# A delta-rule recurrence whose triangular inverse is multiplied into the per-chunk products ahead of the chain of chunks

## Chip, cores and metric

One core of one Trainium2 chip. The metric is the device time of one execution in microseconds; three executions of the kernel before were timed, and a fourth was profiled.

## What is computed

A decoder trunk of two layers over 256 positions of width 1024, float32 in and out. The part that the change touches is the recurrence of layer 0 (8 heads of 64, state `S` of 64 x 64 a head):

```python
def step(S, inp):
    r_t, w_t, k_t, v_t, kk_t, a_t = inp
    sa = jnp.einsum('bhvk,bhk->bhv', S, -kk_t)
    S = (S * w_t[:, :, None, :] + sa[..., None] * (kk_t * a_t)[:, :, None, :]
         + v_t[..., None] * k_t[:, :, None, :])
    return S, jnp.einsum('bhvk,bhk->bhv', S, r_t)
```

The rest of layer 0 is a combined projection, a second mixer (gMLP: a layer norm over the positions' values and a 128 x 128 spatial product), the output projection and a gated feed-forward; layer 1 is attention and another feed-forward.

## The kernel before, in words

Large products run as three matmuls of split operands (`mm3`, tiles `pg`): weights arrive by SP's queue as `raw`, ScalarE makes `whi` (L246), VectorE makes `wlo` (L247). Everything else of TensorE goes to the tiles `pm`.

The recurrence is cut into 4 chunks of 64 positions, in two halves (`h` = 0, 1) of 4 heads each. `stream(h)` builds for each chunk of each head the operands `WR` (128 rows: 64 of the state's and 64 of the values' side; columns 0:64 W0, 64:128 for the outputs, 128:192 for the next state) and `BK` (columns 0:64 A, 64:192 what the solution of the triangular system is multiplied with). The 64 x 64 triangular matrix is inverted in steps: VectorE inverts 16 x 16 blocks (L177 `ftmp`, L690 to L702, tile `xx`) on data that ScalarE's queue carries through DRAM (`scrA`, L670, read back as `at`, L675; written as `scrX`, L701 and L703, read back as `XT`, L706), and the section `lev` joins blocks with four small products (`each`, `low`, L736 to L749; VectorE's COPY_PREDICATED, L742 and L743, and copies on VectorE and ScalarE). `XT`'s second half is `TI`, the inverse transposed.

Then the chain over the chunks `c`, per half: `pw` = W0 times the state, copied to `w0t` (L773); `pq` = inverse times `w0t`, copied to `qst` (L779); `pn`, the next state, from a product over 128 rows and one over 64 rows with `qst`, copied to `SV` (L787, VectorE and ScalarE one half each); `po`, the output, in the same way, copied to `oT` (L792). After every second chunk a side job (`epilogue`, tiles `sqo`, `r2e`) normalises 128 positions.

`projections()` issues the large products of the layer; between a long run of them and the output projection stands the layer norm of the second mixer (tile `vt`, L529 to L538). `drive()` decides in which order TensorE gets all this, by a clock of its own: each job says how much TensorE time a step takes, `RAT` how much of the projections is put behind it, and the table `WAIT` how long each step has to stay away from the one before. TensorE's order is kept as issued (`tc.manual_schedule`); the other engines' orders are made by the scheduler, with `PRI` as its priorities.

Of the kernel before, what the change touches and what calls it, by code (L numbers as in the profile page):

```python
# [8 lines left out]
F32 = mybir.dt.float32  # L9
# [3 lines left out]
OP = mybir.AluOpType  # L13
# [10 lines left out]
DECAY = math.exp(-0.5)  # L24


WAIT = {'s0': [0, 3402, 0, 0, 0, 0, 5130, 0, 0, 6181, 0, 1558, 0, 0, 0, 0, 29481, 1432, 0, 614, 2396, 0, 0, 1233, 677, 0, 0, 451, 317, 0, 0, 0, 98, 638, 0, 377, 334, 316, 0, 0, 528, 1719], 's1': [0, 0, 0, 19323, 0, 0, 2756, 596, 813, 0, 0, 0, 0, 29456, 711, 0, 0, 527, 0, 0, 599, 67, 0, 296, 671, 180, 0, 0, 0, 802, 275, 0, 256, 750, 589, 0, 0, 381, 499], 'v0': [], 'v1': [0, 0, 0, 0, 2188, 540], 'e00': [0, 2221, 997], 'e01': [0, 914, 2924], 'e10': [0, 957, 1874], 'e11': [0, 896, 1993], 'p': [3172, 8550]}
DSQ = (3, 5)
WARM = 16
SEGS = []  # L30
# [2 lines left out]
RAT = {'rows': 3.5, 'pk0': 0.151, 'pk1': 0.1, 'lora': 0.568, 'prod0': 1.61, 'prod1': 0.03, 'v0': 1.318, 'v1': 1.865, 'lev0': 0.3, 'lev1': 0, 'ch0': 0.116, 'ch1': 0}  # L33
# [126 lines left out]
def body(nc, tc, A, out):  # L160
# [3 lines left out]
    V, S, G, PE, SP = nc.vector, nc.scalar, nc.gpsimd, nc.tensor, nc.sync  # L164
# [3 lines left out]
    sm = ctx.enter_context(tc.tile_pool(name="sm", bufs=2))  # L168
# [3 lines left out]
    def mm(o, l, r, start=True, stop=True, shared=False):  # L172
        cnt[0] += 1
        PE.matmul(o, l, r, start=start, stop=stop, skip_group_check=shared)  # L174

    def tt(o, a, b, op, eng=None):
        (eng or V).tensor_tensor(o, a, b, op)  # L177
# [17 lines left out]
    ident, ones = C("ident", 128), C("ones", 1)  # L195
# [155 lines left out]
    def mps():  # L351
        return ps.tile([128, 512], F32, name="pm", tag="m", bufs=5)
# [43 lines left out]
    def layer_even(nxt):  # L396
# [6 lines left out]
        n = norm_new()  # L403
# [13 lines left out]
        WR = ev.tile([128, 2, 16, 192], F32, name="WR")  # L417
# [160 lines left out]
        def stream(h):  # L578
# [127 lines left out]
                    S.dma_start(XT[64 * p:64 * p + 64, w], grid(scrX[h, w], p))  # L706

            yield ("side", f"v{h}", values(h))
            yield ("sec", "lev")
            XI, TI = XT[:, 0], XT[:, 1]  # L710
            YI = chunks(t2("YI"))
# [38 lines left out]
            yield ("pe", 860, RAT[f"lev{h}"])  # L750


            yield ("need", f"val{h}")
            oT = t2("oT")
            YB[h] = [t2(f"yb{i}", F32R) for i in "hl"]

            def heads():
                for j in js:
                    for p in range(2):
                        yield j, p, slice(64 * p, 64 * p + 64), slice(64 * (j - 2 * h), 64 * (j - 2 * h) + 64)  # L760

            def pair(o, whole, half):

                for i, f in enumerate((whole, half)):
                    for j, p, q, e in heads():
                        mm(o[q, e], *f(j, p, q, e), i == 0 and j == js[0], i == 1, True)

            for c in range(4):
                pw = mps()
                for j, p, q, e in heads():  # L770
                    mm(pw[q, e], WR[:, p, 4 * j + c, 0:64], SV[:, p, j, c])
                w0 = sm.tile([128, 128], F32, name="w0t", tag="w0t", bufs=3)
                V.tensor_copy(w0, pw[:, 0:128])  # L773
                yield ("pe", 330, RAT[f"ch{h}"])
                pq = mps()
                for j, p, q, e in heads():
                    mm(pq[q, e], TI[q, 4 * (j - 2 * h) + c], w0[q, e])
                qs = sm.tile([128, 128], F32, name="qst", tag="qst", bufs=3)
                V.tensor_copy(qs, pq[:, 0:128])  # L779
                yield ("pe", 330, RAT[f"ch{h}"])  # L780
                if c < 3:
                    pn = mps()
                    pair(pn, lambda j, p, q, e: (WR[:, p, 4 * j + c, 128:192], SV[:, p, j, c]),
                         lambda j, p, q, e: (BK[q, 4 * j + c, 128:192], qs[q, e]))
                    for p in range(2):
                        q = slice(64 * p, 64 * p + 64)
                        (S.copy if p else V.tensor_copy)(SV[q, p, jsl, c + 1, :], pn[q, 0:128].rearrange("p (j n) -> p j n", j=2))  # L787
                    yield ("pe", 660, RAT[f"ch{h}"])
                po = mps()
                pair(po, lambda j, p, q, e: (SV[:, p, j, c], WR[:, p, 4 * j + c, 64:128]),  # L790
                     lambda j, p, q, e: (qs[q, e], BK[q, 4 * j + c, 64:128]))
                S.copy(oT[:, :, 64 * c:64 * c + 64], po[:, 0:128].rearrange("p (j n) -> p j n", j=2))  # L792
                yield ("pe", 660, RAT[f"ch{h}"])
                if c % 2:
                    yield ("side", f"e{h}{c // 2}", epilogue(h, c // 2, oT))

        def values(h):
            js = (2 * h, 2 * h + 1)
            jsl = slice(2 * h, 2 * h + 2)
            k_ = kx[h]  # L800
            yield ("sec", "val")

            yield ("need", f"v{h}")
            for p in range(2):
                G.memset(SV[64 * p:64 * p + 64, p, jsl, 0, :], 0.0)
            pp = mps()
            for g in range(8):
                j, c = 2 * h + g // 4, g % 4
                for p in range(2):
                    q, o_ = slice(64 * p, 64 * p + 64), slice(64 - 64 * p, 128 - 64 * p)  # L810
                    mm(pp[o_, 64 * g:64 * g + 64], v_[q, j, 64 * c:64 * c + 64], C("cent", 64)[q])
                if g % 4 == 3:
                    yield ("pe", 648, RAT[f"v{h}"])
            pv = pp.rearrange("p (j c n) -> p j c n", j=2, c=4)
            for p in range(2):
                o_ = slice(64 - 64 * p, 128 - 64 * p)
                S.copy(SV[o_, p, jsl], pv[o_])

            pg = mps()
            for i, j in enumerate(js):  # L820
                mm(pg[:, T * i:T * i + T], lora[:, 512 + 128 * j:640 + 128 * j], L[:, 1])
            S.copy(gate[:, jsl], pg.rearrange("p (a b) -> p a b", a=2))
            yield ("pe", 870, RAT[f"v{h}"])

# [397 lines left out]
```

## Time and profile before

| what | us |
|---|---|
| three timed executions | 669.67, 677.36, 678.03 (median 677.36) |
| profiled execution, its own time | 672.47 |
| its span, first to last instruction | 670.6 |
| mean granted TensorE clock of the span | 0.981 |

The span is the time from the first to the last instruction that the profile records; 1.9 us of the profiled execution lie around it. The recurrence runs beside the projections of layer 0, in the first 165 us of the span; what follows it is not touched.

### The profile page before, as it was taken

Reading aid. Unit: us, or ns where it says so; the run is one execution under the profiler, and the core shown is the slowest. Engines: PE = TensorE matmul, PEld = TensorE weight load, DVE = VectorE, ACT = ScalarE, POOL = GpSimd, SP = SyncE. Lnnn points to the kernel's source line nnn. Section 1 sums busy time; section 2 is a strip of 40 time slices with the busy share of each in tenths; the row PEclk is TensorE's granted clock in tenths of the full one; section 3 lists DMA queues with packets and bytes.
Section 4 is the critical chain, followed back from the end, with each engine's and each line's share of the span. In section 5 each row is a group of like instructions: output and inputs, shape, how many; then the busy total and the mean of one; then the engine's idle time right before and its main releaser. Section 6 shows DMA issues by size and latency. Waiting matters only on the chain.

```text
span 670.6 us, 14493 instructions
## 1 busy us (share of the span) xinstructions
PE 642.1 (96%) x5766; PEld 613.1 (91%) x5766; DVE 500.4 (75%) x904; ACT 390.6 (58%) x710; POOL 136.4 (20%) x196
## 2 busy tenths in 40 slices
PE   7998979799899999999999999999999999999995
PEld 6997767679899999999999999999999999998895
DVE  6799967647988888886656479886887888885543
ACT  6776432324666666665445467776576666664431
POOL 4100000110414444441112000001233333331000
PEclk9998999869999999999999999999999999999999
DMA  7747264202456665666666454442755555555541
GB/s 253 249 148 232 71 177 100 73 2 95 127 193 198 197 198 190 189 178 199 188 196 225 160 158 133 139 137 78 245 193 178 189 188 184 185 190 176 179 127 63
DMA packets 44915, 110.33 MB, mean 165 GB/s; under 512 B 16432, under 2 KB 18096, under 8 KB 44848
## 3 DMA queue, kind: packets, MB, share of 16 engines
q1 hardware_dynamic: 31104, 105.03, 48.6%
q10 hardware_dynamic: 13584, 3.86, 2.4%
q8 instruction: 45, 0.74, 0.4%
q0 software_dynamic: 160, 0.52, 0.3%
q14 instruction: 22, 0.18, 0.1%
HBM read 106.50 MB, written 2.90 MB: 163 GB/s over the span
## 4 chain that ended last, share of the span: by engine, by line
PE 79%; DVE 12%; DMA 3%; issue 2%; ACT 1%; POOL 1%; ACTq 1%; SPq 0%; POOLq 0%; DVEq 0%
PE pg L174 63%; PE pm L174 14%; DVE wlo L247 3%; DVE WR L177 2%; DMA scrA<-BK 1%; DVE ftmp L177 1%; PE pm L1142 1%; DVE xl L304 1%; DMA R<-xT 1%; DMA at<-scrA 1%; DMA raw<-w_up 1%; ACTq L706 0%; PE prb L174 0%; DVE BK L662 0%; POOL r L321 0%
## 5 line engine op out<-in xcount | busy, mean ns | idle before, releaser
L246 ACT ACTIVATE whi<-raw 128x1024 fp32r<-128x1024 f32 (+2 forms) x199 | 202.6, 1024 | 157.2 <-PE pg L174 77.6
L174 PE MATMUL pg<-xh,whi 128*128 128x256 f32 x1008 | 289.1, 287 | 0.4 <-ACT whi L246 0.4
L247 DVE TENSOR_TENSOR wlo<-raw,whi 128x1024 fp32r<-128x1024 f32 (+2 forms) x199 | 234.5, 1183 | 71.4 <-ACT whi L246 70.8
L174 PE MATMUL pg<-xh,wlo 128*128 128x256 f32 x1008 | 283.1, 281 | 2.0 <-DVE wlo L247 2.0
L174 PE MATMUL pg<-xl,whi 128*128 128x256 f32 x1008 | 283.1, 281 | 0.1
L174 PEld LDWEIGHTS pg<-xh,whi 128*128 128x128 f32 x1008 | 191.7, 190 | 6.1 <-issue 3.9
L174 PEld LDWEIGHTS pg<-xh,wlo 128*128 128x128 f32 x1008 | 191.5, 190 | 2.7 <-DVE wlo L247 2.6
L174 PEld LDWEIGHTS pg<-xl,whi 128*128 128x128 f32 x1008 | 193.2, 192 | 0.7 <-DVE xl L300 0.3
L177 POOL TENSOR_TENSOR y<-y 128x256 f32<-128x256 f32 x44 | 61.7, 1401 | 27.7 <-ACT y L987 26.8
L177 POOL TENSOR_TENSOR sqacc<-sqacc,sq 128x256 f32<-128x256 f32 x21 | 18.6, 887 | 166.0 <-ACT sq L312 165.5
L984 ACT ACTIVATE y<-z,pc 128x256 f32<-128x256 f32 x88 | 47.5, 587 | 3.3 <-DVE z L177 3.3
L174 PE MATMUL pg<-hh,wlo 128*128 128x256 f32 x176 | 48.6, 276 | 0.0
L174 PE MATMUL pg<-hl,whi 128*128 128x256 f32 x176 | 48.6, 276 | 0.0
L174 PE MATMUL pg<-hh,whi 128*128 128x256 f32 x176 | 48.6, 276 | 0.0
L177 DVE TENSOR_TENSOR z<-pg,rb 128x512 f32<-128x512 f32 (+1 forms) x46 | 30.5, 667 | 21.3 <-PE pg L174 21.3
L985 DVE SCALAR_TENSOR_TENSOR y<-z,pc,y 128x256 f32<-128x256 f32 x88 | 38.6, 478 | 0.8 <-ACT y L984 0.8
L986 DVE SCALAR_TENSOR_TENSOR y<-z,pc,y 128x256 f32<-128x256 f32 x88 | 38.6, 478 | 0.1
L174 PEld LDWEIGHTS pg<-hl,whi 128*128 128x128 f32 x176 | 33.0, 188 | 0.0
L174 PEld LDWEIGHTS pg<-hh,wlo 128*128 128x128 f32 x176 | 33.0, 188 | 0.0
L174 PEld LDWEIGHTS pg<-hh,whi 128*128 128x128 f32 x176 | 33.0, 188 | 0.0
L177 POOL TENSOR_TENSOR hl<-y,hh 128x256 fp32r<-128x256 f32 x42 | 31.2, 742 | 0.0
L975 POOL MEMSET z<- 128x4 f32 x44 | 4.2, 103 | 128.7 <-DVE y L986 97.4
(248 smaller groups left out, 1032.5 us busy)
## 6 DMA issues: line engine op xcount, KB each, us to landing
raw<-w_up SPq DMA_DIRECT2D x88, 512.0 KB, 3.5
raw<-w_dn SPq DMA_DIRECT2D x30, 512.0 KB, 3.5
raw<-w_qkv SPq DMA_DIRECT2D x24, 512.0 KB, 3.5
raw<-w_in SPq DMA_DIRECT2D x20, 512.0 KB, 4.8
raw<-w_dn SPq DMA_DIRECT2D x16, 448.0 KB, 3.4
raw<-ev_wo SPq DMA_DIRECT2D x8, 512.0 KB, 3.8
raw<-od_wo SPq DMA_DIRECT2D x8, 512.0 KB, 4.0
R<-xT SPq DMA_DIRECT2D x4, 256.0 KB, 4.2
```

The lines of the kernel that those rows point to most:

```text
L174: PE.matmul(o, l, r, start=start, stop=stop, skip_group_check=shared)
L177: (eng or V).tensor_tensor(o, a, b, op)
L246: S.activation(hi[:, c], raw[:, c], AF.Copy)
L247: last["lo"] = V.tensor_tensor(lo[:, c], raw[:, c], hi[:, c].bitcast(F32), OP.subtract).ins
L304: V.scalar_tensor_tensor(x[1][:, k], R[:, k], P(gname, k), x[0][:, k].bitcast(F32), op0=OP.mult, op1=OP.subtract)
L975: G.memset(z[:, :, 0:2], 0.0)
L984: S.activation(y[:, g], z[:, g, 2:T + 2], AF.Identity, scale=P(f"cw{l}2", ch), bias=P(f"cb{l}", ch))
L985: V.scalar_tensor_tensor(y[:, g], z[:, g, 1:T + 1], P(f"cw{l}1", ch), y[:, g], op0=OP.mult, op1=OP.add)
L986: V.scalar_tensor_tensor(y[:, g], z[:, g, 0:T], P(f"cw{l}0", ch), y[:, g], op0=OP.mult, op1=OP.add)
L1142: PE.transpose(pt[:, 128 * i:128 * i + 128], sc[:, 128 * i:128 * i + 128], ident)
```

## The change

Per half, each chunk's W0 is transposed on TensorE right after the inverse's data went out (16 products with the identity, four copies on ScalarE). After `lev`, the inverse is multiplied into it (`pu`, 16 products, two copies on VectorE and two on ScalarE), and the result, as the left operand, into `BK[:, 64:192]` (`ph`, 32 products in two groups), whose 16 blocks are added to `WR[:, 64:192]` by 8 instructions of VectorE. In the chain `pw`, `pq` and the 64-row products are gone; a chunk is `pn` and `po`, one product a head over all 128 rows. `WAIT` has new entries for the new steps, and round numbers for those behind them.

```diff
-WAIT = {'s0': [..., 29481, 1432, 0, 614, 2396, 0, 0, 1233, 677, 0, 0, 451, ...
+WAIT = {'s0': [..., 4000, 24381, 1432, 0, 614, 2396, 0, 700, 1000, 0, 1000, 700, ...
...
             yield ("side", f"v{h}", values(h))
+
+            for i in range(2):
+                pt = mps()
+                for g in range(4):
+                    for p in range(2):
+                        mm(pt[64 * p:64 * p + 64, 128 * g:128 * g + 128], WR[:, p, 8 * h + 4 * i + g, 0:64], ident)
+                g4 = slice(8 * h + 4 * i, 8 * h + 4 * i + 4)
+                for a in range(2):
+                    S.copy(WR[:, a, g4, 0:64], pt.rearrange("p (g a t) -> p a g t", g=4, a=2)[:, a])
+            yield ("pe", 1100, 0)
...
+            pu = [mps() for _ in range(2)]
+            for i, cs in enumerate(((0, 1), (2, 3))):
+                for jj in range(2):
+                    for x, c in enumerate(cs):
+                        for p in range(2):
...
+                            mm(pu[i][q, e:e + 128], TI[q, 4 * jj + c], WR[q, 0:2, g, 0:64])
+                for jj in range(2):
...
+                    (V.tensor_copy if jj else S.copy)(WR[:, 0:2, g:g + 2, 0:64].rearrange("p a g t -> p g a t"),
+                        pu[i][:, 256 * jj:256 * jj + 256].rearrange("p (g a t) -> p g a t", g=2, a=2))
+            yield ("pe", 1000, RAT[f"lev{h}"])
+            for cs in ((0, 1), (2, 3)):
+                ph = [mps() for _ in range(2)]
+                for jj in range(2):
+                    for x, c in enumerate(cs):
+                        for a, p in ((0, 0), (1, 1), (1, 0), (0, 1)):
...
+                            mm(ph[p][64 * a:64 * a + 64, e:e + 128], WR[q, a, g, 0:64], BK[q, g, 64:192])
+                for p in range(2):
+                    for jj in range(2):
...
+                        tt(w, w, ph[p][:, 256 * jj:256 * jj + 256].rearrange("p (g n) -> p g n", g=2), OP.add)
+                yield ("pe", 1000, RAT[f"lev{h}"])
...
             for c in range(4):
-                pw = mps()
-                for j, p, q, e in heads():
-                    mm(pw[q, e], WR[:, p, 4 * j + c, 0:64], SV[:, p, j, c])
-                w0 = sm.tile([128, 128], F32, name="w0t", tag="w0t", bufs=3)
-                V.tensor_copy(w0, pw[:, 0:128])
-                yield ("pe", 330, RAT[f"ch{h}"])
-                pq = mps()
-                for j, p, q, e in heads():
-                    mm(pq[q, e], TI[q, 4 * (j - 2 * h) + c], w0[q, e])
-                qs = sm.tile([128, 128], F32, name="qst", tag="qst", bufs=3)
-                V.tensor_copy(qs, pq[:, 0:128])
-                yield ("pe", 330, RAT[f"ch{h}"])
                 if c < 3:
                     pn = mps()
-                    pair(pn, lambda j, p, q, e: (WR[:, p, 4 * j + c, 128:192], SV[:, p, j, c]),
-                         lambda j, p, q, e: (BK[q, 4 * j + c, 128:192], qs[q, e]))
+                    for j, p, q, e in heads():
+                        mm(pn[q, e], WR[:, p, 4 * j + c, 128:192], SV[:, p, j, c])
...
-                    yield ("pe", 660, RAT[f"ch{h}"])
                 po = mps()
-                pair(po, lambda j, p, q, e: (SV[:, p, j, c], WR[:, p, 4 * j + c, 64:128]),
-                     lambda j, p, q, e: (qs[q, e], BK[q, 4 * j + c, 64:128]))
+                for j, p, q, e in heads():
+                    mm(po[q, e], SV[:, p, j, c], WR[:, p, 4 * j + c, 64:128])
...
-                yield ("pe", 660, RAT[f"ch{h}"])
+                yield ("pe", 640, RAT[f"ch{h}"])
```

VectorE, where the block inverse of the second half begins (`at` is its data, read back from DRAM) and the joining of the first half (`XT_872`) needs its COPY_PREDICATED. Before:

```order
L177 TENSOR_TENSOR u<-pg,rb 128x512
L523 SCALAR_TENSOR_TENSOR bw<-pm,pc,bw 128x128 x4
L177 TENSOR_TENSOR v__99<-v__99,pm 128x512
L247 TENSOR_TENSOR wlo<-raw,whi 128x1024 x2
L177 TENSOR_TENSOR ftmp<-xx,at 64x2
L177 TENSOR_TENSOR v__99<-v__99,gate 128x512
L690 TENSOR_REDUCE xx<-ftmp 64x2
L742 COPY_PREDICATED XT_872<-csti,pm 32x8x32
L177 TENSOR_TENSOR ftmp<-xx,at 64x8
L742 COPY_PREDICATED XT_872<-csti,pm 32x8x32
```

Now the block inverse starts right behind `u`, and this is its end:

```order
L177 TENSOR_TENSOR ftmp<-at,xx 64x512
L696 TENSOR_REDUCE z_1180<-ftmp 64x64
L177 TENSOR_TENSOR ftmp<-xx,z_1180 64x512
L247 TENSOR_TENSOR wlo<-raw,whi 128x1024
L699 TENSOR_REDUCE xx<-ftmp 64x8x8
L752 COPY_PREDICATED XT_872<-csti,pm 32x8x32
L702 COPY xx<-xx 64x256
L752 COPY_PREDICATED XT_872<-csti,pm 32x8x32
L753 COPY_PREDICATED XT_872<-csti,pm 128x512
```

The COPY_PREDICATED of the first half moved from the third instruction of the second half's block inverse to behind its last but one.

TensorE, where the projections (`pg`) have run out and the layer norm's product (`pm<-bw,vt`) is still to come. Before, the third chunk of the first half stands here:

```order
L174 MATMUL pg<-whi,xl 128x256
L174 MATMUL pm<-SV,WR 64x64 x4
L174 MATMUL pm<-w0t,XT_872 64x64 x4
L174 MATMUL pm<-XT_1163,BK 64x64 x16
L174 MATMUL pm<-cst,sqo 128x2 x2
L174 MATMUL pm<-SV,WR 64x64 x4
L174 MATMUL pm<-qst,BK 64x64 x4
L174 MATMUL pm<-bw,vt 128x128 x4
L174 MATMUL pm<-cst,r2e 128x128 x2
```

Now the second group of `ph` (`pm<-BK,WR`) and the chain from its first chunk on:

```order
L174 MATMUL pg<-whi,xl 128x256
L174 MATMUL pm<-BK,WR 64x128 x16
L174 MATMUL pm<-SV,WR 64x64 x4
L174 MATMUL pm<-WR,SV 64x64 x4
L174 MATMUL pm<-XT_1185,BK 64x64 x16
L174 MATMUL pm<-SV,WR 64x64 x4
L174 MATMUL pm<-WR,SV 64x64 x4
L174 MATMUL pm<-bw,vt 128x128 x4
L174 MATMUL pm<-SV,WR 64x64 x4
L174 MATMUL pm<-WR,SV 64x64 x4
L174 MATMUL pm<-bw,vt 128x128 x4
```

Two chunks of the chain that stood among the projections before now stand behind them.

## Rows read from the trace of the kernel before

**Rows 1.** The page, part 1: busy time, share of the span and instructions of each engine.

```profile
PE 642.1 (96%) x5766; PEld 613.1 (91%) x5766; DVE 500.4 (75%) x904; ACT 390.6 (58%) x710; POOL 136.4 (20%) x196
```

**Rows 2.** Waits of TensorE: waiting tile, releaser: total us, times, longest us.

```profile
PE pm L174 <- DVE vt L538: 3.5, 1, 3.5
...
PE pm L174 <- DVE w0t L773: 2.2, 3, 1.4
PE pm L174 <- ACT SV L817: 2.0, 1, 2.0
```

**Rows 3.** Timeline of TensorE: start, duration, instruction, count, [idle before].

```profile
118.66 0.45 PE L174 MATMUL pm<-SV,WR 128*64 128x64 f32 x8
...
125.69 1.95 PE L174 MATMUL pm<-bw,vt 128*128 128x128 f32 x8 [3.51 <-DVE vt L538]
...
142.57 0.58 PE L174 MATMUL pg<-xh,whi 128*128 128x256 f32 x1
...
160.29 0.60 PE L174 MATMUL pm<-cst,r2e 128*128 128x128 f32 x4
```

**Rows 4.** Timeline of TensorE: the forms nearest to the added and removed ones.

```profile
42.89 0.88 PE L174 MATMUL pm<-WR,BK 64*64 64x192 f32 x16
43.70 0.39 PE L174 MATMUL pg<-xh,whi 128*128 128x256 f32 x1
...
99.20 1.15 PE L174 MATMUL pm<-XT,YI 64*64 64x64 f32 x32
100.28 0.38 PE L174 MATMUL pg<-whi,xh 128*128 128x256 f32 x1
...
104.99 0.69 PE L174 MATMUL pm<-XT,YI 32*32 32x32 f32 x32
...
112.51 0.45 PE L174 MATMUL pm<-WR,SV 128*64 128x64 f32 x8
112.89 0.45 PE L174 MATMUL pm<-BK,qst 64*64 64x64 f32 x8
...
157.38 0.50 PE L174 MATMUL pm<-cst,sqo 128*128 128x2 f32 x4
...
158.17 0.28 PE L174 MATMUL pg<-xh,whi 128*128 128x256 f32 x1
...
160.17 0.28 PE L174 MATMUL pg<-xh,wlo 128*128 128x256 f32 x1
```

**Rows 5.** VectorE's groups by form, 80 to 165 us: count, busy us, mean ns.

```profile
L773 DVE COPY w0t<-pm 128x128 f32<-128x128 f32 x8 | 2.3, 288 | 5.9 <-PE pm L174 5.9
...
L177 DVE TENSOR_TENSOR oT<-oT,pm 128x256 f32<-128x256 f32 x4 | 1.7, 420 | 3.2 <-PE pm L174 3.2
```

**Rows 6.** Timeline of VectorE: the block inverse of the second half.

```profile
99.56 0.15 DVE L177 TENSOR_TENSOR ftmp<-xx,at 64x2 f32<-64x2 f32 x1 [1.58 <-DMA at<-scrA]
...
100.34 0.43 DVE L742 COPY_PREDICATED XT<-csti,pm 32x256 f32<-32x256 int32 x1
...
110.30 0.37 DVE L702 COPY xx<-xx 64x256 f32<-64x256 f32 x1
```

**Rows 7.** Timeline of ScalarE and its queue: reading the inverse back.

```profile
84.51 3.47 ACTq L706 DMA_DIRECT2D XT<-scrX  x4
88.02 0.58 ACT L817 COPY SV<-pm 64x512 f32<-64x512 f32 x1 [3.69 <-issue]
...
110.22 0.58 ACTq L701 DMA_DIRECT2D scrX<-xx  x1
...
113.39 2.91 ACTq L706 DMA_DIRECT2D XT<-scrX  x4
```

**Rows 8.** Windows: PE, PEld, DVE, ACT, POOL busy, granted clock, DMA share, GB/s.

```profile
126.00:129.00 3.00, 3.00 (x20) 2.70 (x19) 1.08 (x4) 0.00 (x0) 0.00 (x0) 0.50 0.18 68
138.00:141.00 3.00, 3.00 (x39) 2.41 (x36) 1.86 (x4) 0.72 (x2) 0.00 (x0) 0.50 0.00 0
141.00:144.00 3.00, 3.00 (x18) 2.66 (x19) 1.47 (x4) 0.63 (x3) 0.00 (x0) 0.50 0.00 0
```

More of the change, by code (lines that the diff above doesn't have):

```diff
@@ L24 @@
 DECAY = math.exp(-0.5)
-WAIT = {'s0': [0, 3402, 0, 0, 0, 0, 5130, 0, 0, 6181, 0, 1558, 0, 0, 0, 0, 29481, 1432, 0, 614, 2396, 0, 0, 1233, 677, 0, 0, 451, 317, 0, 0, 0, 98, 638, 0, 377, 334, 316, 0, 0, 528, 1719], 's1': [0, 0, 0, 19323, 0, 0, 2756, 596, 813, 0, 0, 0, 0, 29456, 711, 0, 0, 527, 0, 0, 599, 67, 0, 296, 671, 180, 0, 0, 0, 802, 275, 0, 256, 750, 589, 0, 0, 381, 499], 'v0': [], 'v1': [0, 0, 0, 0, 2188, 540], 'e00': [0, 2221, 997], 'e01': [0, 914, 2924], 'e10': [0, 957, 1874], 'e11': [0, 896, 1993], 'p': [3172, 8550]}
+WAIT = {'s0': [0, 3402, 0, 0, 0, 0, 5130, 0, 0, 6181, 0, 1558, 0, 0, 0, 0, 4000, 24381, 1432, 0, 614, 2396, 0, 700, 1000, 0, 1000, 700, 700, 700, 700, 700, 700], 's1': [0, 0, 0, 19323, 0, 0, 2756, 596, 813, 0, 0, 0, 0, 4000, 24356, 711, 0, 0, 527, 0, 700, 1000, 0, 1000, 700, 700, 700, 700, 700, 700], 'v0': [], 'v1': [0, 0, 0, 0, 2188, 540], 'e00': [0, 2221, 997], 'e01': [0, 914, 2924], 'e10': [0, 957, 1874], 'e11': [0, 896, 1993], 'p': [3172, 8550]}
 DSQ = (3, 5)
@@ L750, in stream @@
             yield ("pe", 860, RAT[f"lev{h}"])
+            pu = [mps() for _ in range(2)]
[3 more added lines that the diff above has]
+                        for p in range(2):
+                            q, g = slice(64 * p, 64 * p + 64), 8 * h + 4 * jj + c
+                            e = 256 * jj + 128 * x
+                            mm(pu[i][q, e:e + 128], TI[q, 4 * jj + c], WR[q, 0:2, g, 0:64])
+                for jj in range(2):
+                    g = 8 * h + 4 * jj + cs[0]
+                    (V.tensor_copy if jj else S.copy)(WR[:, 0:2, g:g + 2, 0:64].rearrange("p a g t -> p g a t"),
[6 more added lines that the diff above has]
+                        for a, p in ((0, 0), (1, 1), (1, 0), (0, 1)):
+                            q, g = slice(64 * p, 64 * p + 64), 8 * h + 4 * jj + c
+                            e = 256 * jj + 128 * x
+                            mm(ph[p][64 * a:64 * a + 64, e:e + 128], WR[q, a, g, 0:64], BK[q, g, 64:192])
+                for p in range(2):
+                    for jj in range(2):
+                        g = 8 * h + 4 * jj + cs[0]
+                        w = WR[:, p, g:g + 2, 64:192]
+                        tt(w, w, ph[p][:, 256 * jj:256 * jj + 256].rearrange("p (g n) -> p g n", g=2), OP.add)
+                yield ("pe", 1000, RAT[f"lev{h}"])
             yield ("need", f"val{h}")
@@ L760, in heads @@
                         yield j, p, slice(64 * p, 64 * p + 64), slice(64 * (j - 2 * h), 64 * (j - 2 * h) + 64)
-            def pair(o, whole, half):
-                for i, f in enumerate((whole, half)):
-                    for j, p, q, e in heads():
-                        mm(o[q, e], *f(j, p, q, e), i == 0 and j == js[0], i == 1, True)
             for c in range(4):
-                pw = mps()
-                for j, p, q, e in heads():
-                    mm(pw[q, e], WR[:, p, 4 * j + c, 0:64], SV[:, p, j, c])
-                w0 = sm.tile([128, 128], F32, name="w0t", tag="w0t", bufs=3)
-                V.tensor_copy(w0, pw[:, 0:128])
-                yield ("pe", 330, RAT[f"ch{h}"])
-                pq = mps()
-                for j, p, q, e in heads():
-                    mm(pq[q, e], TI[q, 4 * (j - 2 * h) + c], w0[q, e])
-                qs = sm.tile([128, 128], F32, name="qst", tag="qst", bufs=3)
-                V.tensor_copy(qs, pq[:, 0:128])
-                yield ("pe", 330, RAT[f"ch{h}"])
                 if c < 3:
                     pn = mps()
-                    pair(pn, lambda j, p, q, e: (WR[:, p, 4 * j + c, 128:192], SV[:, p, j, c]),
-                         lambda j, p, q, e: (BK[q, 4 * j + c, 128:192], qs[q, e]))
+                    for j, p, q, e in heads():
+                        mm(pn[q, e], WR[:, p, 4 * j + c, 128:192], SV[:, p, j, c])
                     for p in range(2):
```

## The prediction

> **What bounds the kernel now.** I read the page's busy times first: TensorE is busy 642.1 us of a span of 670.6 [rows 1], so all its idle time is 28.5 us, in the whole kernel. That is the first thing to see: nothing that shortens a chain of waits can be worth more than a part of it, and anything that adds matmuls is paid in full where TensorE has no gap. Next the waits of TensorE [rows 2]: the longest is for the layer norm's `vt` (3.5 us, once); the chain's own waits, for `w0t`, are 2.2 us in three places; the wait for `SV` (2.0) comes before the chain starts. So the chain of the recurrence, which the change shortens, is already hidden nearly everywhere by projections that are put between its steps. Then the timeline of TensorE at the one place where nothing is left to put between [rows 3]: projections end at 118.7, the layer norm's product starts at 125.7, large products start again at 142.6, and the last normalisation product of the recurrence (`r2e`) is at 160.3. From there on the kernel is a row of large products that keep TensorE full, so a shift at that point is a shift of the end. My sum is therefore the place of that `r2e` in the two kernels. Last the clock in windows: the granted clock is 0.50 (1.2 instead of 2.4 GHz) from 126 to 129, behind the 3.5 us of idleness, and again from 138 to 144 [rows 8]; a matmul there costs double.
>
> **TensorE's work.** Removed per half are 60 products: `pw` 16, `pq` 16, and the 64-row parts of `pn` (12) and `po` (16). They come in 15 groups of four; from the start of one group to the next it is 0.38 us (112.51 to 112.89 [rows 4]), so 5.7 us a half. Added are 16 transposing products, 16 of `pu` and 32 of `ph`, all with 128 columns, forms that the trace does not have. In instructions (each product is two) the nearest rows are: 16 of 64x192 that use all four quarters of the array, 0.81 us or 51 ns each; 32 of 64x64 in two quarters, 1.08 us or 34 ns each; 8 of 128 rows, 64 columns, 0.38 us or 48 ns each (from a start to the next start [rows 4]). `ph` is built like the first with two thirds of the columns: 34 to 51 ns, 32 instructions a group, 1.1 to 1.6 us; I take 1.3, twice a half. `pu` is like the second with twice the columns: 34 to 68 ns, 1.1 to 2.2 us; I take 1.8. The transposes are like the third with twice the columns: 48 to 96 ns, 1.5 to 3.1 us; I take 1.9. Together 6.3 us a half (bounds 4.8 and 8.5) against 5.7: TensorE has 1.2 us more to do in both halves together (bounds -1.8 and +5.6). By work alone nothing is won.
>
> **Copies and additions.** VectorE loses 16 copies of 0.29 us (4.6) and gets 16 additions and 4 copies of 128x256 at 0.42 (8.4) [rows 5]; ScalarE gets 12 copies of about the same size (near 5 us). None is on the path by its length; what counts is where they and their neighbours stand.
>
> **Up to the end of the projections (before: 118.7).** (1) On ScalarE the `SV` copies stand behind the reading back of `XT`; its issue takes from 84.5 to 88.0 and the two copies of 0.58 end at 89.2, which is the 2.0 us wait [rows 2, 7]. The transposes of the second half now stand where that wait was. One more `wlo` in front of the block inverse of the first half and copies behind DMAs shift this to about 90.0, and the second eight transposes wait for the copies of the first eight (they get the same buffer): when the projections' next run starts, TensorE is some 3.7 us later than before, 1.9 of it the transposes. (2) The new order on VectorE is the large item. The block inverse of the second half now starts right behind `u`, and its first instruction waits for `at` from DRAM, which landed at 99.6 [rows 6]. So VectorE idles some 4 us, and then does what it did before in that time (`v`, `bw`, a `wlo`) between the steps of the inverse. The inverse ran from 99.6 to 110.3 [rows 6]; it will again take about 11 us, to 111.5 with the shift of 0.8. The COPY_PREDICATED of the first half, at 100.3 before, stands behind it: done at 112.4. TensorE, with 24 large products more behind it than before (0.117 us each: the last two of [rows 4] are 17 products apart), gets there at 107.7: a new wait of 4.7 us. (3) The inverse's result goes out at its end, and ScalarE's queue blocks until it can read it back: from 110.2 to 116.3 before [rows 7], so to 117.5 now. Before, ScalarE's copies for `low` stood ahead of this; now the `YI` and `XT` copies stand behind it. TensorE comes to them near 117.4 (24 large products at 0.117, half of them at the lower clock behind the wait): another 0.5 us. From 117.9: two `low` and `pu` steps 2.8, nine large products 1.05, `ph` 1.3, nine more 1.05: the projections end at 124.2, 5.5 later.
>
> **From there to the last `r2e`.** The layer norm took 7.0 us from the last projection to its product (118.7 to 125.7 [rows 3]); VectorE now has eight additions and two `SV` copies around it, +0.5: product at 131.8. Behind it are: two layer norm products 2.0 (the row's 1.95 for one is at the lower clock), three groups of the first chain 1.2, the second half's `each` 1.1 and three 32x32 groups of 0.69, four `sqo` of 0.50 and four `r2e` of 0.60 [rows 3, 4], `pu` and `ph` 4.4, the second chain's seven groups 2.7, and 78 large products 9.1: 26.9 us, plus 4.0 of waits that I count in the order of the engines (for `r2e` 1.3, for a `YI` copy behind an `r2e` copy 1.7, two small ones 1.0). That is 162.7. Before, the same stretch ends at 160.7, with 12 large products fewer done; with them 162.1. Here is what the change gives: 36.4 us (125.7 to 162.1) become 30.9. But the first is measured with its low clock and the second counted at the full one. In rows 8 the low clock lost half of 9 us, 4.5; I take half of that again, 2.3, with 0 and 4.5 as ends. Sum: 162.7 - 162.1 + 2.3 = +2.9 us.
>
> **To the time.** The profiled execution took 672.5; with +2.9 it is 675.4. It lies 4.9 under the median shown (677.4) and 2.8 over the fastest; the middle of all four executions is 674.9. I forecast the median on that: 678 us.
>
> **A rule from the skill against the change.** An evacuation of 128x256 takes 0.42 us on VectorE [rows 5], and `ph`'s 16 products of 1.3 us need four of them, 1.7 us. The Trainium skill, "TensorEngine Tiling (Array Packing)", section Performance Considerations, says that packing the array speeds up TensorE but not the emptying of PSUM, which may become the bottleneck. The trace agrees in the ratio: 1.7 against 1.3. By that rule the second half's chain would start when VectorE is done with its additions, 8 x 0.42 = 3.4 us behind `ph`'s first group; with 21 large products between (2.5) and the second group (1.3) that is covered, so it gives the same sum unless the additions run twice as long, then about +3.
>
> **Rivals.**
> A, a few us faster: the wait (2) does not come, because `at` lands earlier, or VectorE goes through the inverse in less than its 11 us with no other work in between. Then 4.7 us and the low clock behind it go: 2.9 - 4.7 - 2.3 = -4.1, 671. For it: 36.4 to 30.9 above is a real saving, and the inverse's own instructions are under 7 of its 11 us. Against: the order puts `v`, `bw` and two `wlo` between, and `at` hangs on ScalarE's queue as before.
> B, slower, by 2% at its end: the lower clock through the building of the second half. Place: from the layer norm's product to the second chain, where now `pu`, `ph` and four `r2e` stand in a row of short waits. Of the 26.9 us some 16 lie there; at 1.2 GHz they are 32, of which 4 hide waits: +12 in place of 2.3, so 688; with the added forms at their upper bounds 690. It decides where the granted clock of 132 to 150 is below 0.7. For it: 138 to 144 was at 0.50 with the same kind of small products. Against: it came back by itself before.
> C, the chain's gain is hidden anyway and so is the new wait: only the work of 1.2 us remains, 676.
>
> **How the numbers follow.** Forecast (0 to +8 us) 0.52, A (-9 to 0) 0.23, B (over +8) 0.17, C 0.08. The time is the forecast's, 678. The range takes in A's centre and B's, with the spread of four executions of one kernel (669.7 to 678.0): 669 to 689. 2% of 675 is 13.5 us, about what a measurement of this kernel can tell from no change; half the idle time of the whole kernel would have to go for faster (0.02), and only B with the upper bounds reaches slower (0.06); within 0.92.
>
> **What would show it.** In the changed kernel's profile: a wait of TensorE for VectorE's COPY_PREDICATED of 3 to 6 us near 108 (step 2; if under 1, A); the projections' end at 122 to 126 and the layer norm's product at 129 to 134; the groups 64x128 at 1.1 to 1.6 us for 32 instructions; from the layer norm's product to the last `r2e` about 31 us; granted clock between 0.6 and 0.9 there. No wait for `w0t` or `qst` is left. The prediction is wrong if `r2e` comes before 158 or after 172, or if the time behind it, the feed-forward, changes.

## The result and the profile after

The changed kernel takes 674.91 us, median of 20 executions (669.6 to 681.26), the kernel before on the same chip 671.3 us (20 executions, 664.63 to 679.37). The ratio is 1.0069, 95% interval 1.005 to 1.0088: slower by 0.7%, some 4.6 us, clear of the spread and far under 2%. Ratios here are taken over undisturbed executions and medians over all, so the two don't divide exactly. The profiled execution took 676.82 us, span 675.0, mean granted clock 0.975 (before: 672.47, 670.6, 0.981).

The page, part 1, answers to [rows 1]: TensorE is busy 3.4 us longer and the span is 4.4 us longer, so its idle time has hardly changed.

```profile
PE 645.5 (96%) x5782; PEld 618.3 (92%) x5782; DVE 503.5 (75%) x908; ACT 395.0 (59%) x722; POOL 136.2 (20%) x196
```

The waits of TensorE, beside [rows 2]. The wait for `w0t` is gone, as the change wants; `vt` is shorter; new at the top are ScalarE's join copy `YI` (L756) and `BK` (L663).

```profile
PE pm L174 <- ACT YI L756: 3.2, 2, 2.3
PE pm L174 <- DVE vt L538: 2.6, 1, 2.6
PE pm L174 <- ACT BK L663: 2.3, 1, 2.3
...
PE pm L174 <- ACT SV L837: 1.0, 1, 1.0
PE pm L174 <- DVE XT L752: 0.9, 2, 0.5
```

TensorE's timeline, beside [rows 3, 4]. In order: the second half's transposes, the first half's `low` steps, its `pu` and its two `ph` groups, the first two groups of its chain, the layer norm's product and the last `r2e`.

```profile
89.89 1.09 PE L174 MATMUL pm<-cst,WR 128*64 128x128 f32 x16 [0.97 <-ACT SV L837]
...
91.73 1.83 PE L174 MATMUL pm<-cst,WR 128*64 128x128 f32 x16 [0.75 <-ACT WR L717]
...
109.55 0.69 PE L174 MATMUL pm<-XT,BK 32*32 32x32 f32 x30 [0.49 <-DVE XT L752]
...
113.20 0.24 PE L174 MATMUL pm<-XT,YI 32*32 32x32 f32 x2
115.74 1.03 PE L174 MATMUL pm<-XT,YI 32*32 32x32 f32 x30 [2.30 <-ACT YI L756]
...
117.64 3.70 PE L174 MATMUL pm<-WR,XT 64*64 64x128 f32 x32
...
123.13 1.10 PE L174 MATMUL pm<-BK,WR 64*64 64x128 f32 x32
...
125.42 1.10 PE L174 MATMUL pm<-BK,WR 64*64 64x128 f32 x32
126.46 0.46 PE L174 MATMUL pm<-SV,WR 128*64 128x64 f32 x8
126.74 0.41 PE L174 MATMUL pm<-WR,SV 128*64 128x64 f32 x8
...
132.23 1.50 PE L174 MATMUL pm<-bw,vt 128*128 128x128 f32 x8 [2.56 <-DVE vt L538]
...
166.74 0.71 PE L174 MATMUL pm<-cst,r2e 128*128 128x128 f32 x4 [0.63 <-ACT r2e L874]
```

The 2.30 us wait for `YI` stands at 113.4 to 115.7; `pu` behind it takes 3.70 us. The layer norm's product comes 6.5 us later than before (125.69) and the last `r2e` 6.4 us later; 1.4 us of the latter are 12 large products more that stand ahead of it.

VectorE's timeline, beside [rows 6]: the second half's inverse starts at 97.93, not at 99.56, right behind `u`, for which VectorE waited for TensorE; the first half's COPY_PREDICATED stands at its end.

```profile
97.32 0.69 DVE L177 TENSOR_TENSOR u<-pg,rb 128x512 f32<-128x512 f32 x1 [2.72 <-PE pg L174]
97.93 0.14 DVE L177 TENSOR_TENSOR ftmp<-xx,at 64x2 f32<-64x2 f32 x1
...
108.35 0.42 DVE L752 COPY_PREDICATED XT<-csti,pm 32x256 f32<-32x256 int32 x1
108.67 0.35 DVE L702 COPY xx<-xx 64x256 f32<-64x256 f32 x1
109.06 0.44 DVE L752 COPY_PREDICATED XT<-csti,pm 32x256 f32<-32x256 int32 x1
```

ScalarE and its queue, beside [rows 7]: the read-back of `XT` is issued from 112.38 to 115.23, and the `YI` copy, whose data were ready before, starts right behind it.

```profile
92.61 0.60 ACTq L675 DMA_DIRECT2D at<-scrA  x1
...
108.50 0.58 ACTq L701 DMA_DIRECT2D scrX<-xx  x1
...
112.38 2.85 ACTq L706 DMA_DIRECT2D XT<-scrX  x4
115.33 0.36 ACT L756 COPY YI<-pm 32x256 f32<-32x256 f32 x1 [4.10 <-issue]
```

The windows, columns as in [rows 8]: the granted clock is 0.50 (1.2 instead of 2.4 GHz) right behind the `YI` wait, and 0.72 on the mean from the layer norm's product to the second chain.

```profile
117.00:120.00 3.00, 3.00 (x25) 2.78 (x26) 0.23 (x1) 0.69 (x2) 0.00 (x0) 0.50 0.15 32
120.00:123.00 3.00, 3.00 (x23) 2.67 (x19) 0.85 (x2) 0.53 (x3) 0.00 (x0) 0.56 0.02 5
...
132.00:150.00 18.00, 15.12 (x216) 13.37 (x216) 11.02 (x28) 5.05 (x13) 2.17 (x2) 0.72 0.06 23
```

### The profile page after: what moved, and what is told of

Read it like the earlier page. It is cut to its first block, busy times and chain, and to the rows that moved or that the text cites. A ratio compares the mean times of both kernels' runs of the same rounds, so it can differ in the third digit from the quotient of the medians.

```text
span 675.0 us, 14540 instructions
## 1 busy us (share of the span) xinstructions
PE 645.5 (96%) x5782; PEld 618.3 (92%) x5782; DVE 503.5 (75%) x908; ACT 395.0 (59%) x722; POOL 136.2 (20%) x196
## 4 chain that ended last, share of the span: by engine, by line
PE 77%; DVE 13%; ACT 3%; issue 3%; DMA 2%; POOL 1%; ACTq 1%; SPq 0%; POOLq 0%; DVEq 0%
PE pg L174 61%; PE pm L174 14%; DVE wlo L247 3%; DVE WR L177 2%; DVE ftmp L177 1%; PE pm L1162 1%; ACT whi L246 1%; DVE xl L304 1%; DMA R<-xT 1%; ACTq L706 1%; DMA scrX<-xx 1%; POOL sqacc L177 1%; DMA pc<-pcol 1%; DVE BK L662 1%; POOL r L321 0%
```

## The experiments

All times in one table. Each ratio is to executions of the kernel before in the same session; their medians lie between 670.42 and 672.07. The layer norm's product is its first row in TensorE's timeline of that run. The last column is the start of the large product (`pg`) with 700 others ahead of it, counted in the same timeline; it is behind the whole recurrence in every run and doesn't depend on how many large products stand between.

| kernel | median us (executions) | ratio to before, 95% | layer norm's product | 701st large product |
|---|---|---|---|---|
| before | 671.3 (20) | 1 | 125.69 | 173.22 |
| changed | 674.91 (20) | 1.0069 (1.005 to 1.0088) | 132.23 | 177.96 |
| e2: read-back on GpSimd | 671.52 (12) | 1.0007 (0.9974 to 1.0041) | 125.20 | 171.23 |
| e3: no transposes | 673.34 (12) | 1.0048 (1.0018 to 1.0079) | 128.39 | 174.03 |
| e4: first half new | 680.17 (6) | 1.0129 (1.0086 to 1.0172) | 128.94 | 181.29 |
| e5: second half new | 675.37 (12) | 1.0042 (1.0006 to 1.0078) | 132.63 | 176.79 |
| f2: changed, wait filled | 673.31 (12) | 1.0008 (0.9968 to 1.0048) | 127.87 | 173.80 |
| f3: e2 with three fills | 666.4 (8) | 0.9878 (0.983 to 0.9927) | 127.17 | 168.84 |
| c1: before, read-back on GpSimd | 670.71 (12) | 0.9975 (0.9942 to 1.0007) | 123.74 | 170.52 |
| c2: before, one fill | 669.11 (12) | 0.9967 (0.9925 to 1.0008) | 123.56 | 168.92 |
| c3: before, read-back and fills | 665.58 (12) | 0.9923 (0.9874 to 0.9973) | 123.46 | 166.03 |
| g1: f3, more of both | 663.45 (12) | 0.9933 (0.9888 to 0.9978) | 126.44 | 168.10 |
| h1: g1, no transposes | 667.72 (12) | 0.9933 (0.9893 to 0.9974) | 126.00 | 168.06 |
| g2: g1, `bw` on SP | 662.7 (6) | 0.9895 (0.9835 to 0.9955) | 122.92 | 164.60 |

A place in a trace is that of one execution. The changed kernel, e2, f2 and f3 do the same on TensorE up to the first wait for COPY_PREDICATED, and are there at 108.82, 107.02, 107.01 and 109.00: about 2 us is what one execution's clock can shift.

**Is it the queue? e2.** The four transfers that read the second half's `XT` back go to GpSimd's queue; no computing instruction moves.

```diff
-                    S.dma_start(XT[64 * p:64 * p + 64, w], grid(scrX[h, w], p))
+                    (G if h else S).dma_start(XT[64 * p:64 * p + 64, w], grid(scrX[h, w], p))
```

> The changed kernel, with the four transfers that read the second half's XT back from DRAM issued by GpSimd's queue and not by ScalarE's; the order of the computing instructions stays on every engine. Theory Q (the loss is a queue: ScalarE's halves of the YI and XT joins of the first half stand behind that read-back, TensorE waits 2.3 us for YI near 115.7, and the lower clock behind that wait doubles pu): the wait falls under 0.4 us, pu of the first half takes 1.9 us and not 3.7, the granted clock of 117 to 123 is over 0.9, the projections end at 120.5 to 122 and not at 125.4, and the time falls by 3 to 5 us, to the kernel before within 0.3%. Rival W (the added matmuls are the loss): the time stays within 1 us of the changed kernel, near 1.006 of the kernel before. Rival L (the lower clock comes there whatever the wait): the wait goes but pu still takes over 3 us, the time falls by some 2 us.

In e2's timelines (ScalarE, then GpSimd) the `YI` copy stands at 109.46, ahead of the read-back. In TensorE's waits none for the first half's `YI` is left, `pu` takes 2.35 us, the granted clock of 115 to 121 is 1.00, and the ratio is 1.0007: the changed kernel's loss is gone, to within the 0.3% of the interval.

```profile
109.46 0.37 ACT L756 COPY YI<-pm 32x256 f32<-32x256 f32 x1
```

```profile
111.42 2.76 POOL L706 DMA_DIRECT2D XT<-scrX  x4 [25.31 <-DMA scrX<-xx]
```

Theory Q holds, W falls as an account of the loss, and L falls. Two numbers missed: `pu` takes 2.35 us at the full clock and not 1.9, and the projections end at 118.4 and not at 120.5 to 122, of which 1.8 us is this execution's earlier place.

**Is it the work? e3**, the changed kernel without the loop of the transposes.

```diff
-            for i in range(2):
-                pt = mps()
...
-                    S.copy(WR[:, a, g4, 0:64], pt.rearrange("p (g a t) -> p a g t", g=4, a=2)[:, a])
```

> The changed kernel without the 32 transposing products and their 8 copies: pu reads W0 untransposed, all else stays. Theory W (work is the loss): 2 x 1.9 us go, and the two waits around the second half's transposes: 4 to 5 us faster than the changed kernel, 670 to 671.5, with the time of the join's read-back moving along. Theory Q (the read-back on ScalarE's queue sets the time): TensorE comes earlier to a point that the block inverse and the read-back set; they start where at lands and u is done, so at most the part of 3 us by which u and at come earlier is kept, and the YI wait of 2.3 us grows or stays: 1 to 3 us faster, 672 to 674, the YI wait still 2 to 4 us.

It is still 0.5% slower than before; of the some 4 us of TensorE's work taken out, about 1.4 us show in the time (0.0021 of 671), and the two intervals overlap. Its waits show where the rest went: to `SV` (2.9) where the transposes stood, and to the `XT` join behind the read-back.

```profile
PE pm L174 <- ACT SV L829: 2.9, 1, 2.9
...
PE pm L174 <- ACT XT L751: 2.4, 1, 2.4
```

That is theory Q, with the wait one step later (`XT`, not `YI`).

**One half alone: e4 and e5.** The loops that the change adds stand under `if h == 0` or `if h == 1`, the former chain in the other half, and each half has the `WAIT` entries of its own form.

> The new form in the first half only; the second half keeps the former chain with w0t and qst and the former waits in its table. In the order of the engines ScalarE's YI join now stands ahead of the read-back, its XT join still behind it, and VectorE still does the second half's inverse between. Theory W (each half adds about 0.6 us of work): near 673. Theory Q: a wait for the XT join of 1 to 3 us stays in the first half, with a lower clock under pu: 673 to 676, as slow as the changed kernel or nearly.

> The new form in the second half only; the first half keeps the former chain and the former waits. In the order of the engines ScalarE's YI and XT joins of the first half stand ahead of the read-back again. Theory W: near 673. Theory Q (the loss is the queue in the first half): projections end within 3 us of 118.7 plus the transposes' 1.9, no wait for YI or XT over 0.6 us between 100 and 120, and the time is that of the kernel before or up to 2 us under it, 669 to 672, since the second chain stands where there is little to put between and saves there.

e4 is slower than the changed kernel, beyond the expectation. In its timeline of TensorE the wait for ScalarE's `XT` join inside `pu` is 6.33 us, not 1 to 3: TensorE got there early, and the read-back ended no earlier (its issue at 115.13, in the changed kernel at 115.23).

```profile
116.46 3.67 PE L174 MATMUL pm<-WR,XT 64*64 64x128 f32 x30 [6.33 <-ACT XT L760]
```

e5 is a miss for both theories. There is no wait over 0.3 us for `YI` or `XT` between 100 and 120, as Q said, but it comes out at 1.0042 and its layer norm's product at 132.63. In its timeline the second half's transposes stand behind a wait of 3.34 us for `SV` and partly run at the lower clock, and all four chunks of the first half's former chain but the last output product are now ahead of the layer norm's product. So more than one thing moved, and e5 doesn't price the second half alone: with the joins ahead of the read-back it still loses 0.4%, and what that is made of stays open.

```profile
89.01 1.37 PE L174 MATMUL pm<-cst,WR 128*64 128x128 f32 x16 [3.34 <-ACT SV L875]
...
91.12 1.98 PE L174 MATMUL pm<-cst,WR 128*64 128x128 f32 x16 [0.74 <-ACT WR L718]
```

**Wait and clock apart: f2.** The changed kernel with products of zeros in the `YI` wait (`fill` issues n products of the tile `idle` into a tile that is overwritten next).

```diff
+    def fill(o, n):
+        z = last["idle"]
+        for _ in range(n):
+            mm(o, z[:, 0, 0:128], z[:, 1])
...
                 pp = mps()
+                fill(pp[:, 0:256], n)
...
-            for p, o, pp in low(YI, TI, 0, 32, 32, 0):
+            for p, o, pp in low(YI, TI, 0, 32, 32, 0, 0 if h else 16):
```

> The changed kernel with 16 products of zeros (128x256, 1.9 us in all) put ahead of the first half's second low step, into the place where TensorE waits for ScalarE's YI copy near 113 to 116; nothing else moves. Theory Q with the clock (the wait is set by the read-back on ScalarE's queue, and the lower clock under pu follows from TensorE standing idle there): the step starts near 115.7 as before, but pu takes 1.9 us and not 3.7, and the granted clock of 117 to 123 is over 0.9: 2 to 3.5 us faster than the changed kernel, 671 to 673. Rival (the lower clock comes there whatever TensorE does in the wait): pu over 3 us again, the time within 1 us of the changed kernel. Rival W (added work): 1.9 us slower.

```profile
111.30 2.07 PE L174 MATMUL pm<-idle 128*128 128x256 f32 x16
...
114.06 0.69 PE L174 MATMUL pm<-XT,YI 32*32 32x32 f32 x30 [0.51 <-ACT YI L762]
...
115.25 2.35 PE L174 MATMUL pm<-WR,XT 64*64 64x128 f32 x32
```

The read-back is where it was (issued 3.5 us behind the first wait for COPY_PREDICATED, 110.53, as in the changed kernel), TensorE does more, and `pu` takes 2.35 us instead of 3.70, at a granted clock of 1.00 from 114 to 124; the time goes from 1.0069 to 1.0008. So the lower clock follows from TensorE standing idle there. Counted from that first wait, which takes out where an execution stands, the layer norm's product comes 23.4 us later in the changed kernel, 20.9 in f2 and 18.2 in e2: the clock is about half of what the wait costs.

**The clock behind the projections: f3 and c2.** f3 is e2 with fills of 16, 8 and 4 in three later waits; c2 is the kernel before with 22 at the first of these. In both (16 stands for f3):

```diff
                 pp = mps()
+                if b == 0:
+                    fill(pp[:, 0:256], 16)
                 for g in range(4):
                     mm(pp[:, 128 * g:128 * g + 128], vt[...
```

> The changed kernel with the second half's read-back of XT on GpSimd's queue, and products of zeros (128x256) in three waits behind the projections: 16 ahead of the layer norm's product, 8 ahead of the second half's second low step, 4 ahead of its pu. If the lower clock between 124 and 142 follows from TensorE's waits there: granted clock over 0.9 in 124 to 142 (with the read-back alone moved it was 0.50 to 0.76 in 124 to 133 and 0.55 in 139 to 142), the layer norm's product 1.0 us a group and not 2.07, pu of the second half 1.9 and not 3.6, the last r2e at 155 to 157 and not at 159.6: 666 to 669, faster than both kernels. If VectorE and ScalarE end that stretch anyway, the full clock only makes the waits longer: under 1 us from the kernel with the read-back alone, 670 to 672.

> The kernel before with 22 products of zeros (128x256, 2.5 us) ahead of the layer norm's product, where TensorE waits 3.5 us for vt. If the lower clock behind follows from that wait: granted clock over 0.9 in 126 to 129, the layer norm's product about 1.0 us a group and not 1.95, 1 to 3 us faster than the kernel before, 668 to 670, and the changed kernel's later lower clock is no property of the change. If not: within 1 us of the kernel before.

e2's windows, without the fills, and f3's, with them, show the same stretches at two clocks:

```profile
124.00:133.00 9.00, 7.80 (x100) 7.06 (x102) 3.96 (x12) 1.73 (x5) 0.96 (x2) 0.62 0.16 59
139.00:142.00 3.00, 3.00 (x31) 2.90 (x30) 1.75 (x3) 1.05 (x3) 0.00 (x0) 0.55 0.00 0
```

```profile
124.00:133.00 9.00, 8.21 (x138) 7.37 (x138) 6.41 (x18) 3.28 (x10) 1.73 (x2) 1.00 0.19 61
139.00:142.00 3.00, 3.00 (x59) 2.54 (x55) 2.22 (x6) 1.29 (x3) 0.00 (x0) 1.00 0.02 5
```

f3 is 1.2% faster than the kernel before, and so faster than the changed one too; its last `r2e` is at 157.62, later than the 155 to 157 expected because its layer norm's product came later than e2's (127.17 against 125.20). In c2 the granted clock behind the layer norm's wait is 1.00, where the kernel before had 0.50:

```profile
126.00:129.00 3.00, 3.00 (x84) 2.77 (x86) 2.44 (x8) 1.28 (x3) 0.00 (x0) 1.00 0.02 5
```

Its time is 0.3% lower, with an interval that touches 1, and from 138 to 141 the clock is 0.50 as before. So the kernel before loses its clock behind this wait too; that loss is no property of the change.

**Is the change worth anything without these? c1 and c3.** c1 is the kernel before with e2's edit. c3 is c2 with that edit and 8 products of zeros ahead of the second half's first `pq`.

```diff
                 pq = mps()
+                fill(pq[:, 0:256], 8 * (h == 1 and c == 0))
```

> The kernel before, with the second half's read-back of XT on GpSimd's queue. In that kernel no copy that TensorE waits for stands behind the read-back. Theory Q (what the read-back costs is a matter of the changed order): within 0.2% of the kernel before, 669.5 to 672. Rival (the read-back on ScalarE's queue costs any version some us): 2 us or more faster, and then moving it doesn't undo what the change did.

> The kernel before with all that helped the changed one: the second half's read-back on GpSimd's queue, 22 products of zeros ahead of the layer norm's product and 8 ahead of the second half's first pq, where TensorE waits for w0t and XT. If the change itself is worth something once its waits and the clock are out of the way (theory: 36.4 to 30.9 us between the layer norm's product and the last r2e), this stays 2 us or more over the changed kernel with the same help (666.4 us in its runs): 668 to 670, ratio 0.994 to 0.998. If the help alone was the gain: 665 to 667.5, ratio 0.990 to 0.993, and the change is worth nothing by itself.

c1: 0.9975, interval 0.9942 to 1.0007. No gain is shown, and one of up to 0.6% isn't excluded. c3 is the telling one: 0.9923, as the second reading said, beside f3's 0.9878 and g1's 0.9933. From the layer norm's product to the last `r2e`, c3 takes 29.64 us (123.46 to 153.10), f3 30.45 (127.17 to 157.62), at a granted clock of 1.00. The window of c3:

```profile
123.46:153.10 29.64, 29.45 (x468) 25.84 (x467) 18.81 (x50) 10.19 (x24) 3.02 (x3) 1.00 0.08 25
```

In this stretch the changed kernel does 12 large products more (606 stand ahead of the last `r2e`, 594 in c3; 1.4 us at 0.117). At full clock the stretch is thus worth 31.0 us in the former kernel and 30.45 in the new form, each with the fills that lie in it (8 and 12 products).

**More of the same, and a trap of my own: g1, h1, g2.** g1 adds to f3 a fill of 16 in the wait for `BK` and puts the first half's read-back on GpSimd's queue too; h1 is g1 without the transposes; g2 is g1 with the two loads of `bw` on SP's queue.

```diff
-            G.dma_start(bs_.rearrange("p g t -> p (g t)"),
+            SP.dma_start(bs_.rearrange("p g t -> p (g t)"),
...
-            G.dma_start(wst, A["wsT"])
+            SP.dma_start(wst, A["wsT"])
```

> The changed kernel with the second half's read-back on GpSimd's queue and its three fills, and two things more: the first half's read-back on GpSimd's queue too, so that the SV copies and the transposes' copies of ScalarE don't stand behind it (TensorE waited 1.1 us for SV there), and 16 products of zeros ahead of the last product group of the second half, inside the 2.3 us wait for BK. If both waits and the low clock of 85 to 96 go: 2 to 3 us under the kernel without them, 663.5 to 664.5, ratio 0.983 to 0.986. If VectorE's order sets that place whatever ScalarE does: no change within 1 us, 666 to 667.5.

> The changed kernel with both read-backs on GpSimd's queue and all four fills (663.45 us in its runs, ratio 0.9933), but without the 32 transposing products and their 8 copies; pu reads W0 untransposed. They take 2 x 2.0 us of TensorE in that kernel, with no wait behind them. Theory (with the queue and the clock out of the way the stretch is bound by TensorE's work): 3 to 4.5 us of it are kept, the layer norm's product at 122 to 123.5 and not at 126.44, 659 to 660.5 us, ratio 0.987 to 0.989. Rival (their place is set by VectorE's inverse and by the SV copies there, as the kernel without transposes alone suggested, which gained 1.4 us): 0 to 1.5 us are kept, a wait of TensorE of 2 us or more for SV, XT or at takes their place, 662 to 663.5.

> The changed kernel with both read-backs on GpSimd's queue and all four fills, and the two loads of bw on SP's queue, since on GpSimd's they stand behind the first half's read-back (TensorE waited 2.7 us there for bw near 96.7 with transposes, 6.8 us without). If that wait is a wait for the load alone: no wait of TensorE for bw is left, the layer norm's product comes at 123.5 to 125 and not at 126.44, ratio 0.988 to 0.991 (0.9933 with the wait). If u and the block inverse set VectorE's place there anyway: the wait goes but another takes its place at the joins near 108 to 112, no change over 1 us, ratio 0.992 to 0.994.

g1 missed: its ratio is 0.9933 and not 0.983 to 0.986, no gain over f3 (its own wait of 2.7 us ahead of the product on `bw` is put down to `xx` by the trace). In h1 a single wait took the place of all the work left out; it is at the top of its waits:

```profile
PE pm L174 <- DVE bw L182: 6.8, 1, 6.8
```

The loads of `bw` stand on GpSimd's queue behind the read-back that g1 had moved there; they landed near 94.5 and 95.1, and VectorE's product on them, for which TensorE waited, starts at 95.21: the queue trap of the changed kernel on another engine. So h1 says nothing on what the transposes cost. In g2 no wait for `bw` is left, the layer norm's product comes at 122.92, and with 0.9895 g2 has the lowest median of all, 662.7; its interval overlaps those of f3, g1 and c3.

## Why the prediction was right and wrong

The forecast was "0 to +8 us", +2.9 by its own sum, range 669 to 689. By the measured ratio the change costs 4.6 us; the median is 674.91. The 678 lay 3.1 us high: it put +2.9 on 674.9, the middle of the four executions known then, where twenty have a median of 671.3. So the anchor was 3.6 us too high and the difference too small, by 1.7 us (by 0.7 if the medians are subtracted): that the time came out within 0.5% is in part luck, two errors that work against each other. By its steps:

- **TensorE's work: right in sum, wrong in parts.** The transposes take 1.9 us a half where the clock is full (in g2 32 instructions from 88.40 to the next group at 90.29), as forecast. `pu` takes 2.3 us (in e2 from 112.60 to the next product at 114.88), above my bound of 2.2: two quarters of the array, 71 ns an instruction, about twice the 34 ns of the 64x64 form at twice the columns. `ph` takes 1.04 us a group (123.13 to the large product at 124.17), under my bound of 1.1: with four quarters 32 ns an instruction. Together 6.3 us, as forecast. The groups that are left in the chain follow each other in 0.28 us (126.46 to 126.74), where 0.38 was taken.
- **Step 1: right, slightly undersized.** Transposes at 89.89, forecast 90.0; behind them TensorE is 4.2 us later than before (93.49 against 89.25), forecast 3.7, with a granted clock of 0.62 from 91 to 95.
- **Step 2, the largest term: failed.** A wait of 4.7 us was forecast, 0.9 came. The order of VectorE was read rightly: COPY_PREDICATED does stand at the end of the inverse, which does take about 11 us. What failed is what the inverse waits for and when it starts: 100.4 forecast, for `at`, 97.93 measured. `at` was issued at 92.61 and landed 2.5 us later; what held the inverse was `u` (97.32), which waits for TensorE. The first COPY_PREDICATED ends at 108.77 (forecast 112.4), and TensorE gets there at 108.38 (forecast 107.7). Transfers issued from 86 to 100, before and then after; the last column is the median from issue to landing:

```profile
raw<-ev_wo SPq DMA_DIRECT2D x3, 512.0 KB, 3.9
XT<-scrX ACTq DMA_DIRECT2D x3, 128.0 KB, 6.1
scrA<-BK ACTq DMA_DIRECT2D x2, 128.0 KB, 6.2
at<-scrA ACTq DMA_DIRECT2D x1, 64.0 KB, 4.5
```

```profile
raw<-ev_wo SPq DMA_DIRECT2D x2, 512.0 KB, 3.5
XT<-scrX ACTq DMA_DIRECT2D x3, 128.0 KB, 3.7
scrA<-BK ACTq DMA_DIRECT2D x2, 128.0 KB, 3.2
at<-scrA ACTq DMA_DIRECT2D x1, 64.0 KB, 2.5
```

  One weight load fewer falls among them; that this is the reason is argued, not shown. The forecast took a transfer's landing time as fixed; those on ScalarE's queue differ by a factor of 1.6 to 1.9 between the two traces.
- **Step 3: mechanism right, undersized.** ScalarE's joins behind the read-back were named, at 0.5 us; they cost 2.3. With step 2's wait gone TensorE came at 113.4 and not at 117.4, while the read-back's issue ended only 2.3 us earlier than forecast (115.2 against 117.5). A wait that goes lays bare the next one: steps 2 and 3 together were forecast at 5.2 us and came to 3.2. e2 shows that without this queue's wait the loss is gone.
- **The clock: undersized, and not foreseen ahead of the layer norm.** Between `YI` and the projections' end it cost `pu` 1.35 us (3.70 against 2.35 in f2) and the nine large products behind it 0.8 us (from 121.28 to 123.13, 1.85 us, against 1.05). This and step 3's wait are what e2 takes away. The projections' last product starts at 125.2, forecast end 124.2. Behind the layer norm 2.3 us were forecast; 34.5 us from its product to the last `r2e` against f3's 30.45 are 4.
- **The saving: failed.** The 30.9 us from the layer norm's product on at full clock are nearly what f3 takes, 30.45. But "36.4 us become 30.9" was no saving: c3 shows the former kernel's stretch at 31.0 at full clock. I credited the change with the lower clock of the kernel before, and the 2.3 us set against it took back only a part: 3.2 us were to be saved there, and 1.5 were (34.6 us, with 1.4 for the 12 large products, became 34.5).
- **The sum of steps 1 to 3 and the clock: luck.** The layer norm's product was forecast at 131.8 and came at 132.23. Step 2's wait was 3.8 us shorter than forecast; step 1, step 3's wait and the clock behind it were 0.5, 1.8 and some 2.2 us longer. The place is right because these cancel.
- **The rule from the skill.** Four additions take VectorE 1.41 us against TensorE's 1.04 for the group they empty (timeline of VectorE in the changed kernel):

```profile
125.13 1.41 DVE L177 TENSOR_TENSOR WR<-WR,pm 128x256 f32<-128x256 f32 x4
```

  No wait of TensorE for `WR` from VectorE stands in the changed kernel's list, so they are covered by what stands between. The Trainium skill, "TensorEngine Tiling (Array Packing)", section Performance Considerations, says that packing doesn't speed up the emptying of PSUM; the trace agrees, and in the changed kernel it decides nothing. In e5, where both groups of the second half's `ph` and its chain stand in a row, and VectorE has other work beside them, TensorE does wait for these additions:

```profile
151.09 0.60 PE L174 MATMUL pm<-SV,WR 128*64 128x64 f32 x5 [0.84 <-DVE WR L177]
```
- **Rivals.** A's condition was met, and its time was not: the wait of step 2 did not come, and step 3 took its place. B's condition was nearly met, a granted clock of 0.72 from 132 to 150 where it said below 0.7, but its price was a third: 4 us and not 12. C comes near what the change does by itself: against c3, the 701st large product stands 2.8 us later in f3, which has the same kind of help, and between 2.1 later and 1.4 earlier in g1 and g2, which have more. The ratios of f3, g1 and g2 lie from 0.45% under to 0.1% over c3's, each difference with about 0.7% on either side. The sign of the change by itself stays open. One more thing is untested: `WAIT` has entries like 1233 and 677 for the former steps and round ones (700, 1000) for the new, and no run looked for better ones, so these are the times of one order of the new form and not of its best.

## What to carry to other kernels

Where an engine's queue issued transfers that wait for other transfers, the computing behind them waited too (2.3 us in the changed kernel, 6.3 in e4); ahead of moving work, list for each such issue the copies behind it and who needs them, and put read-backs on a queue with nothing urgent in it (then look at what was in that one: h1). A stretch of waits on TensorE cost more than its waits here, because the clock fell behind them (f2): before crediting a change with a shorter stretch, compare it with the old form at the same clock, and try products of zeros in the waits, which here gave the new form 1.3% (e2 to f3) and the former 0.5% (c1 to c3, where the intervals overlap). A wait that a change takes away or adds is worth only its distance to the next one in the order: 4.7 us forecast in step 2 and 0.5 in step 3 came to 0.9 and 2.3.

## What the runs showed that I had not expected

The same large products, with TensorE and its weight loads busy without a gap and the clock granted in full, run at two paces. Windows of the kernel before and of e2, both in the feed-forward, where the two do the same:

```profile
190.00:280.00 90.00, 90.00 (x797) 90.00 (x796) 76.82 (x116) 62.45 (x101) 37.12 (x50) 1.00 0.60 192
```

```profile
190.00:280.00 90.00, 90.00 (x766) 90.00 (x766) 75.11 (x112) 59.85 (x97) 35.83 (x49) 1.00 0.59 188
```

That is 0.113 us a product against 0.1175. From 190 to 370 e2 and f3 did 1531 of them, the kernel before 1589 and the changed one 1585; 54 at 0.113 are 6.1 us. So e2's profiled span (673.4) is only 1.6 us under the changed kernel's though its 701st large product came 6.7 us earlier. Which pace a stretch has changes from one execution to the next; what decides it was not found. These 6.1 us are more than the whole effect of this change, so single spans say little here.
